# Attention of a hybrid encoder block on one core: score maxima, exponentials and splits issued one slot after their matmuls, queries and keys fetched by head, w_ada sums kept in PSUM

## The chip, the core and the metric

The kernel runs on one core of a Trainium2 chip. The core has a matrix engine (TensorE, PE in the profile; its weight loads are PEld), VectorE (DVE), ScalarE (ACT), GpSimd (POOL), and a queue (SP) from which nearly all transfers are started. Sixteen DMA engines carry those transfers between the chip's memory and SBUF. Matmuls write to PSUM, which VectorE and ScalarE read. The metric is the device time of one execution in microseconds (us), the median over several runs.

## What is computed

One encoder block over a sequence of 1024 positions of width 1024, all in float32. The part that the change bears on is this:

```python
ada = jax.nn.silu(c) @ w_ada[i] + b_ada[i]
shift1, scale1, gate1, shift2, scale2, gate2 = [t[:, None, :] for t in jnp.split(ada, 6, axis=-1)]
h = rmsnorm(x, g_mix[i]) * (1 + scale1) + shift1
proj = h @ w_in[i]
qa, ka, va, qb, kb, vb, ga, gb = jnp.split(proj, split_at, axis=-1)
oa = mixture_of_dilations(heads(qa, 8), heads(ka, 8), heads(va, 8), rel_bias)
ob = neighbourhood_attention_2d(heads(qb, 8), heads(kb, 8), heads(vb, 8), na_rpb[i])
...
merged = jax.nn.sigmoid(ga) * ya + jax.nn.sigmoid(gb) * yb
x = x + gate1 * (merged @ w_out[i])
```

The dilated attention has eight heads of 64. Each query sees a band of keys at three dilations (1, 4 and 16), each band has its own softmax, and the three results are weighted by the denominators of the three. The neighbourhood attention has eight heads of 64 as well: positions form a grid of 16 by 64, and a query sees a window of 8 by 16 with a learned bias. After this come two branch products, w_out, and a gated feed-forward network with a convolution over three positions, w_up and w_down.

## The kernel before

**Numbers.** TensorE multiplies in a reduced float32 format (fp32r in the profile). To keep full precision each operand is split into a high part (a copy, rounded by ScalarE) and a low part (source minus high part, by VectorE or GpSimd), and a product is three matmuls: high by high, high by low, low by high. So a lot of copy-and-subtract pairs surround every matmul.

**Stages up to the attention.** Rows of w_ada are read in pairs and summed with weights on VectorE, to give ada (`row_pairs`, L671 and L673). Each sum runs over eight rows in a tile `sq` in SBUF and is folded by transposes and reductions afterwards. Beside that TensorE forms the values v (`v_wide`, L308 to L310), which go to a scratch in memory. `t_split` (L765 copy, L766 subtraction) splits sums of blocks of h; these are operands of `p_products`, which forms the queries and keys by a block scheme with seven products for eight (L499 to L501). Its operands are weights, split in `a_operands`. The queries and keys, high and low, are stored in a scratch `q_scr` (`qks` in the profile; 8 pairs of heads, 4 kinds, 128 rows for two heads, 1024 positions): L378 for the dilated heads, L396 for the others.

**The attention** is a list of 100 slots. Each slot holds lists of jobs named first, O, T, late O, S, last and W, and `run` issues them in this order; between them `fill` issues steps of another product, the gate projections gA and gB (three matmuls of 512 columns a step, L84 to L86), so that TensorE has work while softmaxes run. `catch_up`, called behind each fill, issues queued small jobs: splits of values (`v_tile`), additions of an output's halves (`finish`, L920 and L921) and splits of gate weights. The instructions of TensorE, ScalarE and VectorE stand in exactly the order in which the code issues them here; SP's and GpSimd's are ordered by a scheduler.

- A **dilated head** takes eight slots from s0. In slots s0 to s0+3 far scores are formed (`far_scores`, L987 and L988, four matmuls, high queries stacked on low ones against keys), in s0+4 to s0+7 near scores (L1027, L1028) that use queries in another order (`qb`, rearranged by GpSimd in `q_blocks`). With the scores, in the same slot, comes the softmax: VectorE takes the maximum (L877), ScalarE the exponential (L878). Two slots later the probabilities P are turned on TensorE (L999, L1044, tile T), and at once split (`split_t`, L885 on ScalarE to `th`, L886 on VectorE to `tl`); another slot later `far_out` and `near_out` (L1011, L1061) multiply them with the values.
- A **pair** of dilated heads shares statistics (maxima and denominators). They are turned, stored to memory, loaded in another shape (`fs`, L1093 and L1099), made into factors (L1105 onwards), stored and loaded again (`fb`, L1134) and multiplied onto the outputs (L1139).
- A **neighbourhood head** takes four slots. Its scores (L1197) are added to a bias that is fetched for each block (`bias`, L1183, two buffers); VectorE takes the minimum of the negated sums (L1201), ScalarE the exponential (L1203); GpSimd divides (L1210), TensorE turns (L1219) and multiplies with the values (L1232).

**Loads of queries and keys.** `qk_load` fetches one pair of heads: per head one transfer for the queries (`qs`, L402, high and low at once) and four for the keys (`ks` and `kl`, L405, each twice so that both halves of the partitions hold them):

```python
sp.dma_start(f(qk[0][i]), q_scr[pr, 0:2, a])
for y in range(2):
    for b in range(2):
        sp.dma_start(f(qk[1 + y][i])[64 * b:64 * b + 64], q_scr[pr, 2 + y, a])
```

Four buffers of each tile hold two pairs. The first pair is fetched before the last product of `p_products` has ended, the others eight slots ahead of their first head, one pair in every 16 slots in the dilated part and one in every 8 in the other.

The slots' loop, with its number of fills, is

```python
n = 2 if s < 64 else 4 if s < 72 else 3 if s < 88 else 2
...
for job in run(slots[s]["T"]):
    job()
...
run(slots[s]["late O"])
run(slots[s]["S"])
```

and is preceded by five fills (`FIRST`). What the jobs of T return are their splits, which so follow their turn in the same slot.

## Time and profile before

| | |
|---|---|
| runs | 1653.1, 1657.18, 1653.93 us |
| median | 1653.93 us |
| the profiled execution, its own time | 1656.75 us |
| its span in the profile | 1654.9 us |
| mean granted TensorE clock | 0.951 |
| memory traffic | 244.27 MB, 148 GB/s over the span |

The profile shows one execution by hardware records. The busy time of an engine leaves out waits and instructions that only steer or start transfers. PEclk is the clock that was granted to TensorE, 1 (or 9 in the page's tenths) being full. In the views of waits a line says which instruction waited, "<-" for whom, and then the sum in us, how often, and the longest wait. In a timeline a row is one instruction: its start in us from the span's start, its duration in us, engine, line, operation, output and inputs, size, and in brackets the wait ahead of it with who ended it. In a group the number behind "x" is the count of instructions, then busy time in us and mean ns of one, then idle time in front of them.

### The profile page before, as it was taken

The page shows a single profiled execution, that of the slowest core. Times are in us where ns is not written, and L with a number is a line of the kernel's source. Part 1 is how long each engine was busy: PE and PEld are TensorE (multiplying, and loading weights), DVE is VectorE, ACT ScalarE, POOL GpSimd, SP SyncE. Part 2 cuts the span into 40 slices and gives each one's busy share as a digit, 9 for nine tenths or more (in the row PEclk, how much of TensorE's full clock was granted, in tenths as well). Part 3 has the DMA queues.
Part 4 walks back from the last instruction along what each step waited for, and adds up shares of the span by engine and source line. Part 5 has one row for each costly group of instructions (what it writes and reads, how often), then busy time and mean ns, then how long its engine had stood idle before and what let it go on. Part 6 is the DMA issues. An engine that isn't in the chain of part 4 may idle for free.

```text
span 1654.9 us, 21287 instructions
## 1 busy us (share of the span) xinstructions
PE 1496.4 (90%) x7308; PEld 1250.3 (76%) x7308; DVE 985.8 (60%) x1805; ACT 782.6 (47%) x1463; POOL 851.8 (51%) x694
## 2 busy tenths in 40 slices
PE   9999999586879568569999999999999999999998
PEld 8877788465767457468888888788888888888888
DVE  7799543143545334346566268966666656977864
ACT  6514332254655444346643455444444443765642
POOL 4066664322433114244222586777766668689723
PEclk9999999798899788879999999999999999999999
DMA  9575354744537566665586342232222223454312
GB/s 371 189 279 183 97 209 148 196 127 121 152 101 173 164 163 149 164 172 162 195 273 229 129 148 93 89 102 77 77 90 77 97 94 121 132 177 134 105 45 102
DMA packets 131187, 244.27 MB, mean 148 GB/s; under 512 B 47460, under 2 KB 60388, under 8 KB 131044
## 3 DMA queue, kind: packets, MB, share of 16 engines
q1 hardware_dynamic: 129080, 239.97, 46.5%
q10 hardware_dynamic: 2000, 2.95, 0.5%
q8 instruction: 58, 0.95, 0.3%
q14 instruction: 49, 0.40, 0.1%
HBM read 188.74 MB, written 59.90 MB: 150 GB/s over the span
## 4 chain that ended last, share of the span: by engine, by line
PE 58%; DMA 22%; DVE 6%; ACT 5%; POOL 4%; issue 2%; SPq 2%; DVEq 0%; ACTq 0%; POOLq 0%
PE pj L499 12%; PE pj L501 12%; PE pj L500 12%; DMA qs<-qks 5%; PE pj L84 5%; PE pj L86 5%; PE pj L85 5%; DMA bias<-na_bias 4%; DMA qks<-qs 2%; DMA gs<-gs 2%; DMA wraw<-w_in 1%; DMA fb<-fcs 1%; DMA sts<-fs 1%; PE O L1232 1%; DVE tl L886 1%
## 5 line engine op out<-in xcount | busy, mean ns | idle before, releaser
L61 POOL TENSOR_TENSOR wlo<-wraw,whi 128x512 fp32r<-128x512 f32 (+1 forms) x92 | 116.7, 1290 | 142.2 <-ACT whi L57 140.4
L886 DVE TENSOR_TENSOR tl<-T,th 128x512 fp32r<-128x512 f32 (+3 forms) x120 | 76.9, 653 | 140.6 <-ACT th L885 140.5
L500 PE MATMUL pj<-op,wsh 128*128 128x512 f32 x408 | 158.7, 389 | 0.5 <-DVE op L1468 0.5
L499 PE MATMUL pj<-op,wsh 128*128 128x512 f32 x408 | 158.4, 389 | 0.3 <-ACT wsh L57 0.3
L501 PE MATMUL pj<-op,wsl 128*128 128x512 f32 x408 | 157.3, 389 | 0.0
L61 POOL TENSOR_TENSOR wsl<-big,wsh 128x512 fp32r<-128x512 f32 (+1 forms) x86 | 111.2, 1315 | 44.4 <-ACT wsh L57 39.4
L84 PE MATMUL pj<-h,whi 128*128 128x512 f32 x272 | 123.5, 454 | 0.0
L86 PE MATMUL pj<-h,wlo 128*128 128x512 f32 x272 | 113.2, 416 | 0.0
L85 PE MATMUL pj<-h,whi 128*128 128x512 f32 x272 | 113.0, 415 | 0.0
L878 ACT ACTIVATE P<-P,st 128x256 f32<-128x256 f32 x128 | 64.1, 501 | 90.6 <-DVE st L877 90.6
L1678 DVE SCALAR_TENSOR_TENSOR big<-pj,sm,big 128x512 f32<-128x512 f32 (+2 forms) x183 | 94.9, 563 | 16.5 <-ACT big L1672 15.5
L1210 POOL TENSOR_SCALAR P<-P,stb 128x288 f32<-128x288 f32 (+1 forms) x32 | 40.5, 1265 | 107.2 <-DVE stb L1207 61.4
L499 PE MATMUL pj<-op,whi 128*128 128x512 f32 x232 | 90.7, 391 | 0.0
L501 PE MATMUL pj<-op,wlo 128*128 128x512 f32 x232 | 90.3, 389 | 0.0
L500 PE MATMUL pj<-op,whi 128*128 128x512 f32 x232 | 90.3, 389 | 0.0
L500 PEld LDWEIGHTS pj<-op,wsh 128*128 128x128 f32 x408 | 76.6, 188 | 16.8 <-DVE op L1468 0.9
L499 PEld LDWEIGHTS pj<-op,wsh 128*128 128x128 f32 x408 | 76.6, 188 | 16.5 <-ACT wsh L57 0.7
L501 PEld LDWEIGHTS pj<-op,wsl 128*128 128x128 f32 x408 | 76.6, 188 | 16.1 <-POOL wsl L61 0.2
L61 POOL TENSOR_TENSOR wsl<-wraw,wsh 128x384 fp32r<-128x384 f32 (+1 forms) x46 | 56.8, 1255 | 57.1 <-ACT wsh L57 52.8
L1203 ACT ACTIVATE P<-P,stb 128x288 f32<-128x288 f32 (+1 forms) x64 | 36.4, 569 | 99.2 <-DVE stb L1201 99.2
L57 ACT ACTIVATE whi<-wraw 128x1024 fp32r<-128x1024 f32 (+2 forms) x49 | 48.5, 994 | 67.9 <-PE pj L85 30.4
L1672 ACT ACTIVATE big<-pj,sm 128x512 f32<-128x512 f32 x61 | 47.0, 772 | 53.3 <-DVE pj L520 32.0
(473 smaller groups left out, 4649.0 us busy)
## 6 DMA issues: line engine op xcount, KB each, us to landing
wada<-w_ada SPq DMA_DIRECT2D x31, 512.0 KB
qks<-qs SPq DMA_DIRECT2D x28, 512.0 KB
wraw<-w_in SPq DMA_DIRECT2D x26, 512.0 KB
big<-w_up SPq DMA_DIRECT2D x22, 512.0 KB
wraw<-w_up SPq DMA_DIRECT2D x22, 512.0 KB
big<-as SPq DMA_DIRECT2D x22, 512.0 KB
as<-big SPq DMA_DIRECT2D x21, 512.0 KB
qs<-qks SPq DMA_DIRECT2D x16, 512.0 KB
```

What stands on the lines that cost most here:

```text
L57: act.activation(hi, raw, AF.Copy)
L61: lo_eng.tensor_tensor(lo[:, i:i + step], raw[:, i:i + step], f(hi)[:, i:i + step], OP.subtract)
L84: pe.matmul(psum, whi[:, k0 + k], mhi, start=k == 0, stop=False)
L85: pe.matmul(psum, whi[:, k0 + k], mlo, start=False, stop=False)
L86: pe.matmul(psum, wlo[:, k0 + k], mhi, start=False, stop=k == n - 1)
L499: pe.matmul(psum, whi[:, k], bhi, start=j < 4 and k == 0, stop=False, skip_group_check=True)
L500: pe.matmul(psum, whi[:, k], blo, start=False, stop=False, skip_group_check=True)
L501: pe.matmul(psum, wlo[:, k], bhi, start=False, stop=k == n - 1, skip_group_check=True)
L878: act.activation(pp, pp, AF.Exp, bias=mi, scale=-1.0, accum_out=li)
L886: dve.tensor_tensor(tl[:m, :n], pt[:m, :n], f(th)[:m, :n], OP.subtract)
L1672: act.activation(y[:, halves[hf]], src, AF.Identity, bias=conv[:, 3, t:t + 1], scale=conv[:, 1, t:t + 1])
L1678: dve.scalar_tensor_tensor(y[:, dst], src, wt, y[:, dst], OP.mult, OP.add)
```

## The change

Seven things are edited, all before or in the attention; the code behind it is the same but for line numbers.

1. **Softmaxes and splits.** `far_scores`, `near_scores` and the neighbourhood's `scores` now put the softmax on a list `scored`, and `split_t` puts its two halves on a list `turned`. `settle`, called at the start of the next slot, issues first the copies to `th`, then the softmaxes, then the subtractions to `tl`. The outputs follow their turn by two slots instead of one, and a slot's order is first, O, T, fill, S, last, fills. There are 102 slots.
2. **Fills.** One ahead of the slots instead of five; then 2 and 3 in turn in a dilated slot (2 before), 3 in slots 64 to 67, 2 up to slot 95, 1 at the end.
3. **Queries and keys by head.** `qk_load` takes one head and allocates one tile each of `qs`, `ks`, `kl` in a new pool with two buffers. It runs eight slots before a dilated head and four before a neighbourhood head (slot 57 for the first of these). The transfers have the same shapes and number. The first head's load, its biases and its values are issued behind all of `p_products`, in an order written out by hand.
4. **Buffers.** P 6 instead of 5, th and tl 5 instead of 3, bias 3 instead of 2.
5. **Values.** A dilated head's values are fetched three slots before it, apart from its bias; a neighbourhood head's two slots into it, and its division comes two slots after its scores.
6. **Sums of w_ada rows.** The running sum stands in a PSUM tile (`pcol` and `pbc` in turn); the eighth addition writes to `sq` in SBUF.
7. **Splits of sums of h.** ScalarE makes a second copy of each source in PSUM (`pj`), from which VectorE subtracts in all 16 cases (GpSimd did four). The first product's operands are prepared in steps 4 to 7 of the loop over v, not behind the splits.

```diff
-    def qk_load(pr):
-        qk = qk_tiles()
-        for i in range(2):
-            a = slice(64 * i, 64 * i + 64)
-            sp.dma_start(f(qk[0][i]), q_scr[pr, 0:2, a])
-            for y in range(2):
-                for b in range(2):
-                    sp.dma_start(f(qk[1 + y][i])[64 * b:64 * b + 64], q_scr[pr, 2 + y, a])
+    def qk_load(head):
+        pr, i = divmod(head, 2)
+        qk = [qk2.tile([128, S], FR, name=n) for n in ("qs", "ks", "kl")]
+        a = slice(64 * i, 64 * i + 64)
+        sp.dma_start(f(qk[0]), q_scr[pr, 0:2, a])
+        for y in range(2):
+            for b in range(2):
+                sp.dma_start(f(qk[1 + y])[64 * b:64 * b + 64], q_scr[pr, 2 + y, a])
         return qk
...
                 if i == 0:
-                    sums[j] = early.tile([128, 512], FT, name="sq", bufs=2)
+                    sums[j] = ps_n.tile([128, 512], FT, name=("pcol", "pbc")[j % 2])
                 for t, w in enumerate(rows.pop(n), 2 * i):
-                    col = cs[:, t:t + 1]
+                    col, acc = cs[:, t:t + 1], sums[j]
+                    if t == KT - 1:
+                        sums[j] = early.tile([128, 512], FT, name="sq", bufs=2)
                     if t == 0:
-                        dve.tensor_scalar(sums[j], w, col, None, OP.mult)
+                        dve.tensor_scalar(acc, w, col, None, OP.mult)
                     else:
-                        dve.scalar_tensor_tensor(sums[j], w, col, sums[j], OP.mult, OP.add)
+                        dve.scalar_tensor_tensor(sums[j], w, col, acc, OP.mult, OP.add)
...
-        PREP = ()
+        PREP = (4, 5, 6, 7)
...
+                prep = [a_operands(raw.pop(0), 4, p_home, p_sts[0], spot=p_spot)]
...
-        def t_split(n, tp, src, eng):
+        def t_split(n, tp, src):
...
+                copy = ps_g.tile([128, 512], FT, name="pj")
+                act.activation(copy, src[k // 2][:, k % 2], AF.Copy)
                 act.activation(t[:, 0], src[k // 2][:, k % 2], AF.Copy)
-                eng[k % 2].tensor_tensor(t[:, 1], src[k // 2][:, k % 2], f(t)[:, 0], OP.subtract)
+                dve.tensor_tensor(t[:, 1], copy, f(t)[:, 0], OP.subtract)
...
+    qk2 = tc.alloc_tile_pool(name="qk2", bufs=2, reuse_waits="tile")
     sm_pool = tc.alloc_tile_pool(name="sm", bufs=2, reuse_waits="tile")
...
+    with tc.manual_schedule(engines={sp.engine, pool.engine}):
+        qks = {0: qk_load(0)}
...
+        biases = {0: dil_bias(0)}
+        values = {0: v_raw(va_load, 0)}
+        biases[1] = dil_bias(1)
...
+        q_blocks(qks[0])
...
-    def split_t(pt, m=128, n=512):
-        th, tl = (at_pool.tile([128, 512], FR, name=x_, bufs=3) for x_ in ("th", "tl"))
-        act.activation(th[:m, :n], pt[:m, :n], AF.Copy)
-        dve.tensor_tensor(tl[:m, :n], pt[:m, :n], f(th)[:m, :n], OP.subtract)
-        return th, tl
-
+    turned, scored = [], []
+
+    def split_t(pt, then, m=128, n=512):
+        def one():
+            tt = [at_pool.tile([128, 512], FR, name=x_, bufs=5) for x_ in ("th", "tl")]
+            act.activation(tt[0][:m, :n], pt[:m, :n], AF.Copy)
+            return tt
+
+        def two(tt):
+            dve.tensor_tensor(tt[1][:m, :n], pt[:m, :n], f(tt[0])[:m, :n], OP.subtract)
+            then(tt)
+        turned.append((one, two))
+
+    def settle():
+        ts = [(one(), two) for one, two in turned]
+        for job in scored:
+            job()
+        for tt, two in ts:
+            two(tt)
+        turned.clear()
+        scored.clear()
+
+    qks[1] = qk_load(1)
...
+                at(s0 - 8, "first", lambda: qks.update({self.head: qk_load(self.head)}))
+            if self.head:
+                at(s0 - 3, "first", self.load_v)
                 at(s0 - 2, "first", self.prepare)
...
                 at(s0 + n, "S", self.far_scores, n)
                 at(s0 + n + 2, "T", self.far_turn, n)
-                at(s0 + n + 3, "late O", self.far_out, n)
+                at(s0 + n + 4, "O", self.far_out, n)
                 at(s0 + n + 4, "S", self.near_scores, n)
...
-                    at(s0 + n + 6, "W" if js == (8,) else "T", self.near_turn, js)
-                    at(s0 + n + 7, "late O", self.near_out, js)
+                    at(s0 + n + 6 + (js == (8,)), "T", self.near_turn, js)
+                    at(s0 + n + 8 + (js == (8,)), "O", self.near_out, js)
...
+            at(57 if head == 0 else s0 - 4, "first", lambda: qks.update({8 + head: qk_load(8 + head)}))
+            at(s0, "first", self.begin)
+            at(s0 + 2, "first", self.load)
+            at(s0 + 4, "last", self.prepare)
...
-                at(s0 + n + 1, "first", self.normalise, cb)
+                at(s0 + n + 2, "first", self.normalise, cb)
...
-    fill(FIRST)
-    for s in range(100):
-        n = 2 if s < 64 else 4 if s < 72 else 3 if s < 88 else 2
+    fill(1)
+    for s in range(102):
+        n = 2 + s % 2 if s < 64 else 3 if s < 68 else 2 if s < 96 else 1
+        settle()
         run(slots[s]["first"])
         run(slots[s]["O"])
...
+        run(slots[s]["T"])
+        fill(n > 1)
         run(slots[s]["S"])
         run(slots[s]["last"])
-        fill(n > 3)
-        for job in run(slots[s]["W"]):
-            job()
-        fill(1)
+        fill(n - (n > 1))
```

Three places of the order show what moves. The first is TensorE in the middle of a dilated head. T are turned probabilities, pj a fill, O an output, S scores. Before:

```order
L999 MATMUL T<-idt,P 128x128 x4
L84 MATMUL pj<-h,whi 128x512
L85 MATMUL pj<-h,whi 128x512
L86 MATMUL pj<-h,wlo 128x512
L1011 MATMUL O<-th,vv 128x256
L1011 MATMUL O<-tl,vv 128x256
L1011 MATMUL O<-th,vv 128x256
L1011 MATMUL O<-tl,vv 128x256
L1027 MATMUL S<-ks,qb 128x256
L1028 MATMUL S<-kl,qb 128x256
```

and now:

```order
L1034 MATMUL O<-th,vv 128x256
L1034 MATMUL O<-tl,vv 128x256
L1034 MATMUL O<-th,vv 128x256
L1034 MATMUL O<-tl,vv 128x256
L1022 MATMUL T<-idt,P 128x128 x4
L84 MATMUL pj<-h,whi 128x512
L85 MATMUL pj<-h,whi 128x512
L86 MATMUL pj<-h,wlo 128x512
L1049 MATMUL S<-ks,qb 128x256
L1050 MATMUL S<-kl,qb 128x256
```

Output O before was that of the turn T issued one slot earlier; now it is that of a turn two slots earlier and stands at the slot's head.

The second place is the queue SP where the projections end and the attention begins. qks<-qs are stores of queries and keys, qs, ks and kl<-qks the loads, vv the values of a head. Before:

```order
L378 DMA qks<-qs 128x2x512
L402 DMA qs<-qks 128x1x1024 x2
L378 DMA qks<-qs 128x2x512
L65 DMA wraw<-w_in 128x1024
L405 DMA kl<-qks 64x1024
L405 DMA ks<-qks 64x1024 x2
L405 DMA kl<-qks 64x1024
L405 DMA ks<-qks 64x1024 x2
L405 DMA kl<-qks 64x1024 x2
L378 DMA qks<-qs 128x2x512
L851 DMA lnm<-ln_mult 128x384
```

and now:

```order
L375 DMA qks<-qs 128x2x512 x2
L65 DMA wraw<-w_in 128x1024
L375 DMA qks<-qs 128x2x512 x2
L399 DMA qs<-qks 128x1x1024
L402 DMA ks<-qks 64x1024 x2
L402 DMA kl<-qks 64x1024 x2
L849 DMA lnm<-ln_mult 128x384
L692 DMA bias<-p_bias 128x512
L693 DMA bias<-p_bias 128x384
L680 DMA vv<-v 128x8x64
```

One head is loaded instead of two, behind the last store instead of between the stores; the second head's load comes after both heads' biases.

The third place is VectorE among the sums over rows of w_ada (mt is the fold that follows a sum):

```order
 L190 TENSOR_REDUCE mt<-idt 128x32
-L671 TENSOR_SCALAR sq<-wada,cs 128x512
-L673 SCALAR_TENSOR_TENSOR sq<-wada,cs,sq 128x512 x7
+L670 TENSOR_SCALAR pcol<-wada,cs 128x512
+L672 SCALAR_TENSOR_TENSOR pcol<-wada,cs,pcol 128x512 x6
+L672 SCALAR_TENSOR_TENSOR sq<-wada,cs,pcol 128x512
 L181 STREAM_TRANSPOSE mt<-sq 128x512
 L185 TENSOR_REDUCE mt<-mt 128x16
```

Seven additions of eight rows read and wrote a tile in SBUF; now all seven read PSUM, six of them write it, and the seventh writes SBUF.

More of the change, by code (lines that the diff above doesn't have):

```diff
@@ L362, in hybrid_encoder @@
     q_scr = dram.tile([8, 4, 128, S], FT, name="qks")
-    def qk_tiles():
-        return [[qkpool.tile([128, S], FR, name=n) for _ in range(2)] for n in ("qs", "ks", "kl")] + [[]]
     def split_qk(y, dst, src):
@@ L840, in hybrid_encoder @@
                 next(nxt, None)
-            if n + 1 == len(order) and j == 2:
-                qk = qk_load(0)
     first_w = w_split(ahead.pop(24), pool)
-    for i in range(2):
-        q_blocks(qk, i)
     ps.release()
@@ L848, in hybrid_encoder @@
     lpool.release()
+    qkpool.release()
+    qk2 = tc.alloc_tile_pool(name="qk2", bufs=2, reuse_waits="tile")
     sm_pool = tc.alloc_tile_pool(name="sm", bufs=2, reuse_waits="tile")
-    lnm = sm_pool.tile([128, 384], FT, name="lnm", bufs=1)
-    sp.dma_start(lnm, ln2_mult)
-    loads = [dil_loads(head) for head in range(2)]
+    with tc.manual_schedule(engines={sp.engine, pool.engine}):
+        qks = {0: qk_load(0)}
+        lnm = sm_pool.tile([128, 384], FT, name="lnm", bufs=1)
+        sp.dma_start(lnm, ln2_mult)
+        biases = {0: dil_bias(0)}
+        values = {0: v_raw(va_load, 0)}
+        biases[1] = dil_bias(1)
+        pool.tensor_tensor(biases[0][:, 512:896], biases[0][:, 512:896], lnm, OP.add)
+        q_blocks(qks[0])
     ps_l = tc.alloc_tile_pool(name="psl", bufs=2, space=PSUM, reuse_waits="tile")
     ps_a = tc.alloc_tile_pool(name="psa", bufs=2, space=PSUM, reuse_waits="tile")
-    def finish_o(po, dst):
-        act.activation(dst, po[64:128], AF.Copy)
-        dve.tensor_tensor(dst, po[0:64], dst, OP.add)
     def block_chunks(b):
@@ L1016, in near_scores @@
         def near_scores(self, n):
-            qs, ks, kl, qb = qks[self.pr]
+            ks, kl, qb = qks[self.head][1:]
             i, st = self.i, self.st()
             s = ps_l.tile([128, 512], FT, name="S")
-            P = sm_pool.tile([128, 2, 256], FT, name="P", bufs=5)
             for x_ in range(2):
@@ L1162, in __init__, with begin @@
                 at(s0 + n, "S", self.scores, cb)
-                at(s0 + n + 1, "first", self.normalise, cb)
+                at(s0 + n + 2, "first", self.normalise, cb)
             for n, pair in enumerate(((0, 3), (1, 2))):
-                s = s0 + 3 + 2 * n
+                s = s0 + 4 + 2 * n
                 for y in range(3):
                     at(s + (y == 2), "T", self.turn, pair, y)
-                at(s + 2, "O", self.out, pair)
+                at(s + 3, "O", self.out, pair)
+        def begin(self):
+            self.st = at_pool.tile([128, 2, 8], FT, name="stb", bufs=3)
         def load(self):
@@ L1172, in load @@
                 oTs[self.head // 2] = at_pool.tile([128, S], FT, name=("u1", "u23")[self.head // 2 % 2])
-            self.st = at_pool.tile([128, 2, 8], FT, name="stb")
             self.vv = v_raw(vb_load, self.head)
@@ L1274, in fill_steps @@
             w = w_next
-    def qk_ahead(pr):
-        qks[pr] = qk_load(pr)
-    qks, oTs = {0: qk}, {}
-    loads = dict(enumerate(loads))
+    oTs = {}
     for pr in range(4):
@@ L1284, in hybrid_encoder @@
         NaHead(head, 64 + 4 * head)
-    for n, cb in zip((52, 55, 59, 61), (0, 3, 1, 2)):
+    for n, cb in zip((54, 56, 59, 61), (0, 3, 1, 2)):
         at(n, "first", vb_chunks, cb)
-    for pr in range(1, 8):
-        at(16 * pr - 8 if pr < 5 else 8 * pr + 24, "first", qk_ahead, pr)
     steps = fill_steps()
```

140 lines of the change are left out of this document (67 added, 73 removed).

## The prediction

> **What bounds the kernel now.** I read the page's summary and slices first, then the busy times of a few stretches, then who waits for whom on each engine, and last the timeline around the longest waits.
>
> ```profile
> PE 1496.4 (90%) x7308; PEld 1250.3 (76%) x7308; DVE 985.8 (60%) x1805; ACT 782.6 (47%) x1463; POOL 851.8 (51%) x694
> ...
> PE   9999999586879568569999999999999999999998
> ...
> PEclk9999999798899788879999999999999999999999
> DMA  9575354744537566665586342232222223454312
> GB/s 371 189 279 183 97 209 148 196 127 121 152 101 173 164 163 149 164 172 162 195 273 229 129 148 93 89 102 77 77 90 77 97 94 121 132 177 134 105 45 102
> ```
>
> TensorE is the busiest engine and is full from slice 20 on. It is open in slices 8 to 19, where its clock falls too and the DMA share is highest. Those slices are the end of the projections and the attention. The same in microseconds (columns: stretch, its length, then busy time and instructions of each engine, clock, DMA share, GB/s):
>
> ```profile
> core 0: us, PE busy (x) PEld busy (x) DVE busy (x) ACT busy (x) POOL busy (x), PEclk, DMA share, GB/s
> ...
> 276.00:310.00 34.00, 21.91 (x98) 17.86 (x96) 4.77 (x7) 1.95 (x4) 8.87 (x10) 0.86 0.53 147
> 310.00:593.00 283.00, 214.46 (x1207) 179.02 (x1207) 122.56 (x397) 148.04 (x406) 78.30 (x72) 0.88 0.57 149
> 593.00:747.00 154.00, 103.00 (x538) 88.21 (x538) 62.76 (x185) 61.45 (x164) 49.78 (x45) 0.81 0.60 158
> 747.00:800.00 53.00, 49.91 (x312) 43.84 (x311) 33.19 (x102) 35.73 (x96) 29.49 (x26) 0.99 0.59 179
> 800.00:1655.00 855.00, 845.11 (x3868) 702.49 (x3866) 574.12 (x881) 415.86 (x606) 535.15 (x436) 0.99 0.37 122
> ```
>
> The borders are those of the program, seen in the first score matmul of a stage and in two of the waits:
>
> ```profile
> 309.86 0.55 PE L987 MATMUL S<-ks,qs 128*128 128x256 f32 x1 [12.09 <-DMA ks<-qks]
> 322.97 1.39 PE L999 MATMUL T<-idt,P 128*128 128x128 f32 x4 [7.55 <-ACT P L878]
> 592.69 0.29 PE L1197 MATMUL S<-ks,qs 128*128 128x288 f32 x1
> 746.99 0.29 PE L1197 MATMUL S<-ks,qs 128*128 128x288 f32 x1
> ```
>
> Slot 0 of the attention begins at 309.86, slot 64 (first neighbourhood head) at 592.69, and counting score matmuls, four to a slot, slot 84 at 746.99. So 64 dilated slots take 283 us, 20 neighbourhood slots 154 us (31 us a head), and the last 16 slots 53 us (3.3 us each, 13 us a head). What comes after 800 us holds TensorE at 845 of 855 us; the change does not touch it. TensorE's own waits in the attention:
>
> ```profile
> PE S L1197 <- DVE stb L1201: 36.3, 5, 10.4
> PE O L1011 <- ACT th L885: 19.0, 3, 7.1
> PE O L1061 <- DVE tl L886: 18.7, 7, 11.1
> PE O L1061 <- ACT th L885: 13.5, 2, 12.7
> PE S L987 <- DMA ks<-qks: 12.1, 1, 12.1
> PE T L1044 <- ACT P L878: 10.7, 1, 10.7
> PE T L999 <- ACT P L878: 8.0, 4, 7.6
> ```
>
> Together 118 us, in few pieces of 5 to 13 us. In between, slots flow. VectorE and ScalarE, which are named, are idle more than half of this time, so their own work is not what is late. What they wait for:
>
> ```profile
> DVE P L1201 <- DMA bias<-na_bias: 60.5, 8, 13.8
> DVE u L1139 <- DMA fb<-fcs: 22.4, 6, 11.5
> DVE fl L1105 <- DMA fs<-sts: 19.4, 3, 7.2
> ...
> 375.81 0.60 ACT L1269 ACTIVATE gs<-pj 128x512 f32<-128x512 f32 x1 [12.20 <-DMA gs<-gs]
> ...
> SPq L695 <- DMA qs<-qks: 40.6, 4, 11.0
> SPq L1183 <- DMA qs<-qks: 26.3, 3, 8.9
> ```
>
> All are transfers, and the queue SP that issues them stood still for one kind, qs<-qks. That transfer is slow by itself:
>
> ```profile
> 346.00:356.00 10.00, 8.68 (x54) 7.16 (x53) 5.60 (x18) 5.94 (x19) 5.79 (x6) 1.00 0.13 50
> ...
> qs<-qks SPq DMA_DIRECT2D x16, 512.0 KB
> ```
>
> Here it runs nearly alone: 50 GB/s at a DMA share of 0.13, that is 2 of 16 engines. Its 512 KB so take 10.5 us on two engines, and whatever is spread over all 16 ends behind it on these two. **The bound of the attention is this pair of DMA engines**, 16 times 10.5 us plus their part of the rest.
>
> [...]
>
> **The change, part by part.**
>
> *Score maxima, exponentials and splits one slot later.* No instruction is added; P tiles go from 5 to 6, th and tl from 3 to 5. The chains PE S, DVE, ACT, PE T and PE T, ACT, DVE, PE O get a slot each. What the edit can remove is waiting for short chains; what it cannot remove is TensorE's work. That is 214.46 x 0.88 / 64 = 2.95 us of full clock a dilated slot with two fills. A fill is three matmuls; their price:
>
> ```profile
> 1160.00:1200.00 40.00, 40.00 (x178) 33.14 (x177) 25.53 (x40) 16.79 (x21) 28.04 (x22) 1.00 0.24 80
> ```
>
> 40 us / 178 = 0.225 us each, 0.67 us a fill. The new schedule has 2.5 fills in a dilated slot instead of 2, so its floor is 2.95 + 0.34 = 3.29 us, 64 x 3.29 = 211 us.
>
> Of the dilated 283 us, 189 are TensorE's work (64 x 2.95) and about 54 are long waits: 22.4 for fb, 19.4 for fs, 12.2 for gs. The other 40 are low clock and short waits. Afterwards I put: 211 work; 20 of the short waits (half; bounds 0 and 40); fs 9 and fb 18. The gs wait goes, as it came from two qs loads back to back, which loading by head does not give. Sum 258, a gain of **25 us**. Why fs and fb stay: the transfers of the pair's statistics are as before, and their chain is long:
>
> ```profile
> 401.21 0.47 SPq L1093 DMA_DIRECT2D sts<-fs  x1
> ...
> 407.51 2.88 SPq L1099 DMA_DIRECT2D fs<-sts  x8
> ...
> 411.63 0.18 DVE L1105 TENSOR_TENSOR fl<-fs 64x32 f32<-64x32 f32 x1 [7.18 <-DMA fs<-sts]
> ```
>
> From issue to use 10.4 us. The rows are now copied a slot later while factors stays at slot 20, so the lead is about 2.5 slots, 8 us, where it was 3.4. 3 us of wait a pair remain even if no qs load is ahead. An fb wait is a wait in VectorE's queue: behind it stand all maxima and splits, and TensorE is held one slot later than now.
>
> *Queries and keys by head.* The same 16 loads with the same bytes, two buffers of each tile instead of four, 8 slots ahead (4 in the neighbourhood stage). Now four heads are fetched before slot 64, so that only four loads fall in the 154 us; afterwards seven fall in slots 64 to 88. The bias has three buffers and its reader comes a slot later. Floor on the two hot engines for a dilated head: share 0.57 x 283 = 161 us, less ten qs loads (10 x 10.5 x 2/16 = 13), over 8 heads 18.5, plus 10.5 = 29 us, 233 us for eight: below my 258. For a neighbourhood head: from the last stretch 0.59 x 53 / 4 = 7.8, plus the 1 MB of ks and kl (3.8 us at the 279 GB/s of the page's third slice, which is full of spread loads), plus 10.5 = 22 us; from the stretch before, (0.60 x 154 - 6) / 5 + 10.5 = 28 us, with the fills and statistics it held. I take 24, the last stretch's row being nearer in fills. Seven heads at 24 and ten slots at 3.3 make 201, plus 2 us of slack at the last loads; now 207 (592.69 to 800). With VectorE's 60.5 us of bias waits gone in part but more loads, I count **6 us** of gain. Bounds: 187 (22 a head) and 229 (28 a head).
>
> *Start.* The first pair's loads no longer stand ahead of the last qks stores, and one head (one hot load) comes before slot 0 instead of two. Of the waits of 12.09 and 7.55 us I take half, **9 us**; bounds 0 and 19. POOL's q blocks fall from eight to four there.
>
> *Sums of w_ada rows and splits in PSUM.* 42 additions read their running sum from PSUM, 16 splits a copy that ScalarE makes there.
>
> ```profile
> L673 DVE SCALAR_TENSOR_TENSOR sq<-wada,cs,sq 128x512 f32<-128x512 f32 x42 | 48.9, 1164 | 4.7 <-DMA wada<-w_ada 3.3
> ...
> L766 DVE TENSOR_TENSOR op<-qs,op 128x512 fp32r<-128x512 f32 x6 | 8.2, 1412 | 0.0
> ...
> L208 DVE SCALAR_TENSOR_TENSOR pv<-wada,cs,pv 128x512 f32<-128x512 f32 x6 | 4.5, 753 | 0.1
> ...
> L886 DVE TENSOR_TENSOR tl<-T,th 128x512 fp32r<-128x512 f32 x54 | 37.3, 691 | 83.6 <-ACT th L885 83.6
> ...
> 100.90 0.76 PE L309 MATMUL pv<-vwl,h 128*128 128x512 f32 x1 [3.79 <-DVE vwl L61]
> 139.49 0.50 PE L308 MATMUL pv<-vwh,h 128*128 128x512 f32 x1 [2.89 <-ACT vs L315]
> ```
>
> With a PSUM operand the same operations take 753 and 691 ns instead of 1164 and 1412: VectorE saves 42 x 0.41 + 11 x 0.72 = 25 us, less four splits taken over from GpSimd (3 us). TensorE waited only these two times longer here, so at most 7 us come out; I take **4**. The 16 copies (about 0.6 us each, 10 us) lie in ScalarE's idle time of that stage; without that cover they would cost the 10. The first product's operands, which are now prepared during the v products (steps 4 to 7) and not behind the splits, add no instruction; GpSimd and ScalarE do them beside TensorE's v products, and I take nothing, between the 3.8 us of the longer wait above either way.
>
> [...]
>
> Sum: 25 + 6 + 9 + 4 = 44 us. The profiled execution took 1656.75 us (span 1654.9), so 1612.75; the three runs have their median 2.8 us lower, at 1653.93, and I give **1610 us**.
>
> **The rivals.**
>
> *Floor of the hot engines* (pipelining pays fully): dilated 233, neighbourhood 187, 19 + 7 at the edges: 50 + 20 + 26 = 96 us, 1558. For it: the 40 us of short waits are what the edit aims at. Against it: statistics chains and eight transfers at most ahead of SP keep the hot engines from being always fed.
>
> *The loads do not bind* (each hides in eight slots): 211 + 20 and 38 x 3.3 = 125: 52 + 82 + 13 = 147 us, 1507. Against it stands the DMA share of 0.13 at 50 GB/s.
>
> *Just in time becomes too late, slower than before.* Two buffers and a lead of four slots, 13 us, cannot hold a load that needs 10.5 us on engines with other work in line. Should a neighbourhood head with its own load take the 31 us of today's, seven of them and ten slots make 250 us, 43 more than now; it decides from 31 - 13 = 18 us of waiting a head. With dilated slots gaining 15 (the same lateness on vv, three slots ahead and behind a qs load) and 9 + 4 at the edges the time is 1654 + 15 = 1669. For it: L1201's waits, which are of this kind. Against it: three bias buffers and a later reader.
>
> *The waits only move*: dilated slots trade 25 us for 15 in fb and fs, no gain in the neighbourhood stage, 13 at the edges: 1630.
>
> **How the numbers follow.** Forecast 1610 with its own range 1590 to 1622: 0.42. Floor of the hot engines 1558: 0.18. Loads do not bind 1507: 0.07. Waits only move 1630 (to 1648): 0.17. Late loads: 0.16, a fifth of it within 5 us of no change. About 0.3%, 5 us, is what a measurement here can tell from no change. So faster 0.81, same 0.06, slower 0.13. Leaving out the two ends, the range is 1548 to 1655.
>
> **What would show it.** Right: first dilated score near 300 us, dilated stage near 258 us, VectorE's waits on na_bias halved, L672 near 750 ns, and SP still standing at qs<-qks. Wrong: neighbourhood heads at 31 us or at 13, waits on fs or fb that grow beyond 40 us, ScalarE held by vv, or time lost after the attention, where I expect the same 855 us.

## The result and the profile after

The changed kernel takes 1638.18 us (median of 4 runs, 1636.94 to 1639.49) against 1654.04; the ratio is 0.9901, with an interval of 0.9884 to 0.9918. It is faster by 16 us, about 1%, where 44 us were forecast. The profiled execution took 1637.79 us (span 1635.6), 19 less than that of before. Its summary and slices:

```profile
PE 1477.8 (90%) x7308; PEld 1248.2 (76%) x7308; DVE 961.3 (59%) x1809; ACT 791.8 (48%) x1479; POOL 838.7 (51%) x690
...
PE   9999998578989846567999999999999999999998
...
PEclk9999999789989867878999999999999999999999
DMA  9584445554644757665776441222222223444312
```

TensorE is open in slices 7 to 19 (8 to 18 before), and the clock is low in nearly the same places. The borders of the stages, from TensorE's timeline (first score of a dilated head, first of a neighbourhood head, last output):

```profile
302.06 0.55 PE L1006 MATMUL S<-ks,qs 128*128 128x256 f32 x1 [19.95 <-DMA ks<-qks]
562.10 0.29 PE L1225 MATMUL S<-ks,qs 128*128 128x288 f32 x1
...
787.50 0.28 PE L1267 MATMUL O<-tl,vv 128*128 128x128 f32 x1
```

and the busy times between them (columns as in the prediction):

```profile
core 0: us, PE busy (x) PEld busy (x) DVE busy (x) ACT busy (x) POOL busy (x), PEclk, DMA share, GB/s
673.70:753.30 79.60, 50.19 (x288) 44.50 (x289) 32.95 (x103) 34.90 (x95) 27.78 (x25) 0.80 0.64 167
562.00:787.50 225.50, 145.33 (x815) 127.97 (x814) 97.37 (x290) 96.45 (x258) 76.85 (x68) 0.80 0.59 153
302.00:562.00 260.00, 220.84 (x1294) 194.19 (x1295) 122.24 (x397) 149.51 (x411) 85.58 (x81) 0.91 0.55 151
```

The last output before came at 809.07 us:

```profile
809.07 0.28 PE L1232 MATMUL O<-tl,vv 128*128 128x128 f32 x1
```

| us | before | after | gain |
|---|---|---|---|
| TensorE empty ahead of slot 0 (start of the wait for the first keys) | 297.8 | 282.1 | 15.7 |
| that wait | 12.1 | 20.0 | -7.9 |
| dilated stage, first score to first neighbourhood score | 282.8 | 260.0 | 22.8 |
| neighbourhood stage, to the last output | 216.4 | 225.4 | -9.0 |
| the rest | 845.8 | 848.1 | -2.3 |

The sum is 19.3, the difference of the two spans. Of the 15.7 us, 2.7 are four fills of 0.67 us that now lie in the slots. The neighbourhood stage, forecast to gain, lost; from first score to first score its seven heads took 27.4, 35.6, 26.0, 28.8, 26.9, 26.6 and 26.9 us, 198 in all. TensorE's, VectorE's and SP's largest waits show where:

```profile
PE T L1254 <- DVE tl L890: 57.8, 8, 11.8
PE T L1022 <- DVE tl L890: 21.2, 6, 7.9
PE S L1006 <- DMA ks<-qks: 20.0, 1, 20.0
```

```profile
DVE P L1235 <- DMA bias<-na_bias: 88.9, 9, 13.0
```

```profile
SPq L774 <- DMA qs<-qks: 32.0, 5, 8.7
```

VectorE's waits for the bias, which were to be halved, grew from 60.5 to 88.9 us. TensorE waits for a split (tl), but the split only stands in VectorE's queue behind a sum that waits for its bias. The bias has not come because SP stood still ahead of it. SP's queue during one head (start, duration, transfer):

```profile
677.60 0.55 SPq L399 DMA_DIRECT2D qs<-qks  x1
678.20 0.47 SPq L402 DMA_DIRECT2D ks<-qks  x1
678.72 1.23 SPq L402 DMA_DIRECT2D kl<-qks  x2
680.05 0.53 SPq L1213 DMA_DIRECT2D bias<-na_bias  x1
680.67 0.38 SPq L65 DMA_DIRECT2D wraw<-w_in  x1
681.28 2.06 SPq L1213 DMA_DIRECT2D bias<-na_bias  x1
683.43 14.39 SPq L774 DMA_DIRECT2D vv<-v  x4
697.92 2.52 SPq L1213 DMA_DIRECT2D bias<-na_bias  x2
```

The slow load of the queries is issued at 677.6, and SP stands at the loads of values from 683 to 698, with the next two biases behind. Of these 14.4 us, 8.7 (the longest in the line above) are a wait for the queries to land, 17.5 us after their issue. VectorE's wait is three links from its cause.

### The profile page after: what moved, and what is told of

It reads as the page before. It is cut to its first block, busy times and chain, and to the rows that moved or that the text cites. A ratio compares the mean times of both kernels' runs of the same rounds, so it can differ in the third digit from the quotient of the medians.

```text
span 1635.6 us, 21337 instructions
## 1 busy us (share of the span) xinstructions
PE 1477.8 (90%) x7308; PEld 1248.2 (76%) x7308; DVE 961.3 (59%) x1809; ACT 791.8 (48%) x1479; POOL 838.7 (51%) x690
## 4 chain that ended last, share of the span: by engine, by line
PE 45%; DVE 3%; POOL 2%; ACT 1%; issue 1%; DMA 1%; DVEq 0%; SPq 0%; POOLq 0%; ACTq 0%
PE pj L496 10%; PE pj L497 10%; PE pj L498 10%; PE pj L86 5%; PE pj L84 4%; PE pj L85 4%; POOL wlo L61 0%; POOL wsl L61 0%; DMA oraw<-w_ada 0%; ACT whi L57 0%; DVE op L1598 0%; DMA wraw<-w_down 0%; DVE wlo L61 0%; PE pcol L108 0%; ACT op L1597 0%
## 5 line engine op out<-in xcount | busy, mean ns | idle before, releaser
L1697 DVE SCALAR_TENSOR_TENSOR big<-pj,sm,big 128x512 f32<-128x512 f32 (+2 forms) x183 | 94.9, 563 | 16.5 <-ACT big L1691 15.5
L875 DVE CUSTOM_DVE_ANT_0 P<-S,bias 128x256 f32<-128x256 f32 x128 | 49.1, 420 | 85.9 <-PE S L1007 36.3
L1235 DVE CUSTOM_DVE_ANT_0 P<-S,bias 128x288 f32<-128x288 f32 (+1 forms) x64 | 30.3, 506 | 114.3 <-DMA bias<-na_bias 88.9
L1254 PE MATMUL T<-idt,P 128*96 128x128 f32 (+1 forms) x192 | 33.9, 312 | 68.9 <-DVE tl L890 57.8
```

Source lines behind the costliest of these rows:

```text
L875: dve.tensor_tensor_reduce(pp, d, bias, -1.0, BIG, OP.add, OP.min, mi)
L1697: dve.scalar_tensor_tensor(y[:, dst], src, wt, y[:, dst], OP.mult, OP.add)
```

## The experiments

Stages are read as in the table above, each from one profiled execution; ratios are to the kernel before, with intervals.

| run | what differs | us | ratio | first score | dilated | neighbourhood |
|---|---|---|---|---|---|---|
| before | | 1654.0 | 1 | 309.9 | 282.8 | 216.4 |
| after | | 1638.2 | 0.9901 | 302.1 | 260.0 | 225.4 |
| e1 | after, queries spread | 1516.3 | 0.9161 (0.9139 to 0.9184) | 291.9 | 214.5 | 157.7 |
| e2 | before, queries spread | 1547.0 | 0.9353 (0.9339 to 0.9368) | 296.6 | 226.9 | 170.0 |
| e3 | after, 3 load buffers, 8 slots ahead | 1645.3 | 0.9937 (0.9912 to 0.9962) | 303.0 | 275.0 | 217.5 |
| e4 | after, splits in their slot | 1633.6 | 0.9876 (0.9855 to 0.9898) | 303.9 | 253.9 | 224.1 |
| e5 | after, early part undone | 1647.9 | 0.9965 (0.9951 to 0.9978) | 314.1 | 258.3 | 222.6 |
| e6 | after, splits of h undone | 1639.8 | 0.9916 (0.9890 to 0.9943) | 304.3 | 258.4 | 222.4 |
| e7 | before, calls by head | 1656.4 | 1.0017 (0.9998 to 1.0036) | 305.9 | 285.4 | 215.0 |
| e8 | e1, splits in their slot | 1518.1 | 0.9177 (0.9153 to 0.9201) | 291.1 | 209.5 | 163.7 |
| e9 | e4, outputs one slot earlier | 1637.5 | 0.9891 (0.9859 to 0.9924) | 302.5 | 264.6 | 217.9 |
| e10 | after, 2 bias buffers | 1641.5 | 0.9916 (0.9886 to 0.9945) | 301.7 | 256.6 | 231.6 |
| e11 | e1, 14 fills first | 1522.8 | 0.9198 (0.9171 to 0.9226) | 292.7 | 211.7 | 166.5 |
| e12 | e1, 3 load buffers, 8 slots ahead | 1513.9 | 0.9142 (0.9109 to 0.9175) | 291.9 | 214.7 | 158.3 |
| e13 | after, fills of before | 1627.2 | 0.9822 (0.9792 to 0.9851) | 303.1 | 244.8 | 225.4 |
| e14 | before, fills of after | 1652.1 | 0.9993 (0.9973 to 1.0014) | 308.5 | 284.3 | 206.0 |
| e15 | 4 load buffers | 1676.3 | 1.0133 (1.0104 to 1.0163) | 302.4 | 288.2 | 231.4 |
| e16 | e1, fills of before | 1505.9 | 0.9092 (0.9069 to 0.9116) | 292.0 | 194.9 | 165.6 |
| e17 | e15 with 2 load buffers | 1665.9 | 1.0069 (1.0047 to 1.0092) | 303.0 | 262.1 | 246.7 |
| e18 | after, th and tl 4 | 1637.4 | 0.9904 (0.9868 to 0.9940) | 303.8 | 258.0 | 224.2 |

**The slow transfer (e1, e2).** The one load of queries is cut into two of 64 partitions:

```diff
-        sp.dma_start(f(qk[0]), q_scr[pr, 0:2, a])
+        for x_ in range(2):
+            sp.dma_start(f(qk[0])[64 * x_:64 * x_ + 64], q_scr[pr, x_, a])
```

> The changed kernel, but the queries of a head come in two transfers of 64 partitions x 1024 (high, low), as the keys do, instead of one whose source has two rows outermost. Bytes are the same, 16 transfers more. Theory (the two busy DMA engines bound the attention: SP stood 42 us at qs<-qks in the neighbourhood stage, a head took 26.5 us there): a neighbourhood head falls to 16 to 18 us (DMA share 0.6 x 26.5 = 16), the dilated stage from 260 to 215 to 230 us, the wait for the first keys from 20 to 12 us; together 1530 to 1565 us. Rival (two buffers and a lead of four slots are too short whatever the transfer's speed): heads stay over 23 us and the time over 1615 us.

> The kernel before with the same edit of the queries' transfer alone. Theory (two busy engines): its waits for bias, fb, fs and gs, 115 us together, mostly go: 1550 to 1590 us. By the rival that the splits' order holds the kernel before: over 1630 us. Beside the changed kernel with the same edit it shows what the change is worth without the slow transfer: 20 to 40 us if the slots' order pays by itself, under 10 us if the change only dealt with the slow transfer.

Measured: 122 us less in the changed kernel, 106 in the one before, more than either expectation. Windows of e1 ahead of slot 0 and in the dilated stage:

```profile
284.00:292.00 8.00, 0.09 (x1) 0.12 (x1) 0.00 (x0) 0.00 (x0) 0.00 (x0) 0.75 0.97 241
291.90:506.40 214.50, 208.79 (x1294) 185.18 (x1295) 124.94 (x397) 148.50 (x412) 85.77 (x81) 0.99 0.74 188
```

The first loads run at a DMA share of 0.97, where the slow load by itself had 0.13; TensorE is busy in 209 of 214.5 us at a clock of 0.99. In the changed kernel, which keeps the transfer's shape, the load is as slow as before: from 294 to 302 us, ahead of slot 0, the DMA share is 0.14 at 55 GB/s. The two stages are 45.5 and 67.7 us shorter than in the changed kernel. So this load, on its two engines (0.13 of 16), held back the attention in both kernels. These two runs don't tell how much of that is the two engines being full and how much is SP standing until the load has landed, since the spread transfer ends both. Without the slow load the change is worth 30.6 us, nearly twice what it is with it.

**Lead and buffers in the neighbourhood stage (e3, e10).**

```diff
-    qk2 = tc.alloc_tile_pool(name="qk2", bufs=2, reuse_waits="tile")
+    qk2 = tc.alloc_tile_pool(name="qk2", bufs=3, reuse_waits="tile")
...
-            at(57 if head == 0 else s0 - 4, "first", ...
+            at((55, 58, 64)[head] if head < 3 else s0 - 8, "first", ...
```

> The changed kernel with three buffers of qs, ks, kl and the neighbourhood heads' loads eight slots ahead instead of four (th and tl have 4 buffers for 5 to make room). Theory (two busy engines, and SP's queue standing at their landing with values and bias behind): heads stay at 25 to 28 us and the time within 6 us of 1638. Rival (the lead of four slots is too short): heads at 16 to 20 us, 1580 to 1600 us.

> The changed kernel with two buffers of the bias instead of three. Theory (the neighbourhood heads run at the pace of the two busy DMA engines, whose 26.5 us a head no bias buffer changes): neighbourhood stage within 6 us of 225, time 1632 to 1645. Rival (the third bias buffer is what kept the heads from the 30 us that they took before): heads at 29 to 31 us, time 1655 to 1670.

In e3 the third to sixth heads still take 26 to 29 us, and only the seventh, whose load is done, takes 15.5. A longer lead doesn't help these heads. It moves a load (ten instead of nine start there) into the dilated stage, which grows by 15 us; the time, 7 us longer, lies just outside the theory's 6. With two bias buffers the time moves by no more than the intervals allow; from the third on, heads take 27 to 29 us, and the stage, 231.6 us, is a little over the 6 us that the theory allowed it.

**The slot's order (e4, e8, e9).** e4 settles in the slot itself; e9 also puts the outputs of the dilated heads one slot behind their turn.

```diff
-        settle()
         run(slots[s]["first"])
         run(slots[s]["O"])
         run(slots[s]["T"])
+        settle()
         fill(n > 1)
         run(slots[s]["S"])
+        settle()
```

> The changed kernel, but maxima, exponentials and splits follow their matmuls in the same slot again (settled behind T and behind S); everything else, the outputs two slots after their turn too, stays. Theory (the later slot took the short waits away): the dilated stage goes from 260 back to 275 to 283 us, and the time to 1653 to 1665 us. Rival (loads by head made the 23 us): dilated stage within 5 us of 260, time within 8 us of 1638.

> The changed kernel with the queries' transfer spread over 64 partitions twice, and maxima, exponentials and splits in the slot of their matmuls again. Theory (the later slot pays once the slow transfer is gone, since short chains are then what TensorE waits for; 12 us in the dilated stage between the two kernels with spread queries): dilated stage 222 to 230 instead of 214.5 us, time 1526 to 1540 instead of 1516 us. Rival (the later slot pays nothing here either): within 5 us of 1516.

> The changed kernel with the slot's order of the kernel before: maxima, exponentials and splits in the slot of their matmuls, and a dilated head's outputs one slot behind their turn, between the fill and the scores. Theory (the outputs' second slot took the short waits away, since undoing the place of the splits alone changed nothing): dilated stage 270 to 283 us, time 1650 to 1662. Rival (no part of the slots' order counts; fs waits 6 instead of 19 us and no gs wait come from the loads' order and the longer slots): dilated stage within 6 us of 257, time 1630 to 1644.

In time all three came out by the rival; e9's dilated stage, 264.6 us, lies 2 us above the rival's bound, and e4's, 253.9, 1 us below it. Settling one slot later, the edit that the title names first, is worth nothing that can be measured, with the slow load or without it.

**The early part (e5, e6).** e5 has the removed lines of `row_pairs` and `t_split` and `PREP = ()` again, e6 those of `t_split` and `PREP` alone.

> The changed kernel with the early part undone: sums of w_ada rows in SBUF, splits from SBUF (a quarter on GpSimd), the first product's operands prepared behind the splits. Theory (the projections ended 13.0 us earlier by this part and the wait for the first keys, 20.0 us, is counted from their end): TensorE runs empty at 295 instead of 282 us, time 1648 to 1654 us. Rival (the prediction's 4 us are right, and the rest came from the first pair's loads no longer standing between the stores): TensorE empty at 284 to 288, time 1640 to 1645 us.

> The changed kernel with the splits of sums of h and the early preparation undone, the sums of w_ada rows still in PSUM. Theory (5.3 us of the 13.0 had come by the end of the products with the values, the other 7.7 in the first products, by the splits and the early preparation): TensorE empty at 288 to 291 us, time 1643 to 1648 us. Rival (the sums alone make the 13 us, the splits nothing): empty at 282 to 284, time 1636 to 1640 us.

In e5 TensorE runs empty at 314.1 - 20.7 = 293.4 us, 11.3 later than in the changed kernel, and the time is 9.7 us longer, six tenths of what the change brings. In e6 it runs empty at 284.0. The sums make 9.4 of the 11.3 us. The other 1.9 can't be put down to the splits and the preparation: the runs that have them, with one fill ahead of slot 0, run empty at 281.9 to 283.9 us. e6 came out by its rival, and e5 within 2 us of its theory.

**Loads by head in the kernel before (e7).** Only the slots of the calls were changed.

> The kernel before, but queries and keys fetched by head at the slots of the changed kernel (eight ahead, in the neighbourhood part four, slot 57 for its first head), with its four buffers; the first pair stays as it was. Theory (the sixteen slow transfers only change stages: eight instead of ten fall in the dilated slots): the dilated stage falls from 283 to 260 to 268 us, the neighbourhood stage grows from 216 by 5 to 20 us, time within 10 us of 1654. Rival (loading by head leaves the dilated stage as it was, the changed kernel's 23 us come from its order of slots): dilated stage over 277 us.

This one did not do what it says: SP's order is made by the scheduler, which starts a load when a buffer is free. The sixteen loads started at nearly the same times as before (325, 332, 380, 411 us against 328, 335, 383, 413). It tells nothing of loading by head; buffers had to be changed for that.

**Fills (e13, e14, e11, e16).**

```diff
-    fill(1)
+    fill(5)
...
-        n = 2 + s % 2 if s < 64 else 3 if s < 68 else 2 if s < 96 else 1
+        n = 2 if s < 64 else 4 if s < 72 else 3 if s < 88 else 2 if s < 99 else 0
```

> The changed kernel with the fills of the kernel before (5 ahead, 2 in a dilated slot, then 4, 3, 2). Theory (longer slots hide the statistics' way through memory: VectorE's waits for fs 6 to 10 us instead of 19): fs waits return to 15 to 22 us and the dilated stage stays at 255 to 265 us although 28 fills fewer lie in it; with those fills in the neighbourhood stage the time is 1640 to 1652 us. Rival (the dilated stage is TensorE's work and a fixed number of waits): dilated stage 238 to 248 us, neighbourhood stage longer by what was moved, time within 6 us of 1638.

> The kernel before with the fills of the changed one (1 ahead, 2 and 3 in turn in dilated slots, 3 in slots 64 to 67, then 2). Theory (longer slots hide the statistics' way): fs waits 5 to 12 instead of 19 us, dilated stage 270 to 283 us with 28 more fills in it, neighbourhood stage 195 to 210, time 1635 to 1648. Rival (fills change places only): dilated stage 295 to 305 us, neighbourhood stage 195 to 205, time within 6 us of 1654.

In e13 the dilated stage has 32 fills fewer (128 against 160) and is 15.2 us shorter; four of them stand ahead of slot 0 and 28 in the neighbourhood stage, which has the same 225.4 us. The first is the rival's forecast, the second neither's, and the time lies below both. So in the changed kernel fills are free where heads wait for the slow load, and cost most of their time in the dilated stage: moving them forward cost the change 11 us. In the kernel before (e14) it was the other way: the dilated stage had room for them (284.3), the neighbourhood stage got 10 us shorter in the profile, and the time did not move beyond its interval, as its rival had it. VectorE's waits for fs in the dilated stage are 8.6 us in e13 and 18.4 in e14, so longer slots aren't what shortens them.

> The changed kernel with the spread transfer of the queries, and 14 fills instead of 1 ahead of slot 0, taken from slots 64 to 67 and 87 to 95. Theory (TensorE stands idle for 9.0 us for the first keys, which 13 fills of 0.67 us cover, and the later slots wait for transfers and not for fills): 1507 to 1513 instead of 1516 us. Rival (what is filled ahead is missing behind, where short chains then show): 1514 to 1520 us.

> The changed kernel with the spread transfer of the queries and the fills of the kernel before (5; 2 in a dilated slot; 4, 3, 2). Theory (the dilated stage is TensorE's work, 28 fills of 0.67 us fewer shorten it by 15 to 19 us, while the neighbourhood heads wait for transfers part of their time and take in about half of them): dilated stage 195 to 200, time 1500 to 1510. Rival (without the slow transfer fills cost the same everywhere): 1513 to 1520.

Fills ahead of slot 0 (e11) took the wait for the first keys away, but the neighbourhood stage grew by 9 us, all of it from the last head on, where 9 fills stand for 12 and TensorE waits 7.5 us for values; the time, 1522.8 us, is no better than e1's and above both expectations. Fewer fills in dilated slots (e16) made 1505.9 us, 132 less than the changed kernel and the lowest of all. e12, with a longer lead on top of e1, expected

> The changed kernel with the spread transfer, three buffers of qs, ks, kl and the neighbourhood heads' loads eight slots ahead (th and tl have 4 buffers). Theory (with the slow transfer gone the first neighbourhood heads, 25 and 26 us against 15 to 16 later, are held by transfers that crowd there at a DMA share of 0.84, which an earlier load spreads): neighbourhood stage 145 to 152 instead of 158 us, time 1504 to 1512. Rival (they are held by the fb and values transfers, which this doesn't move): within 5 us of 1516.

and is no different from e1 within the intervals; the rival was right.

**What shortened the dilated stage (e15, e17, e18).** e15 has four load buffers and pairs' loads; to make room P, th, tl and bias have their old numbers and the slots their old order. e17 is e15 with two load buffers and loads by head, so these two differ in both. e18 is e3's partner: it has e3's four buffers of th and tl, but the changed kernel's load buffers and lead.

> The changed kernel with four buffers of qs, ks and kl and a pair's two loads at the slots of the kernel before; to make room P has 5 buffers, th and tl 3, the bias 2, and maxima, splits and outputs stand in the slots of the kernel before. Only the early part, the fills, the start and the order of the values' loads stay as changed. Theory (two buffers hold a slow load back until a pair's statistics are through; four let it start ahead of them): dilated stage 272 to 285 us, neighbourhood stage 205 to 218. Rival (the count of buffers doesn't matter): dilated stage 255 to 266 us, neighbourhood stage 218 to 228.

> The kernel of e15 with two buffers of qs, ks and kl and the loads by head at the changed kernel's slots; P, th, tl, bias and the slots' order as in e15. Theory (the load buffers decide): dilated stage 255 to 266 us, against 288 in e15; time 1640 to 1655. Rival (the smaller buffers of P, th and tl decide): dilated stage 278 to 292 us, time 1665 to 1680.

> The changed kernel with th and tl at 4 buffers. Theory (the load buffers decide): dilated stage 255 to 264 us as with 5, against 275 in e3; time within 5 us of 1638. Rival (th and tl decide): dilated stage 270 to 278 us.

First neighbourhood score of e15 and of e17, whose first dilated scores stand within 0.6 us of each other:

```profile
590.63 0.29 PE L1225 MATMUL S<-ks,qs 128*128 128x288 f32 x1
```

```profile
565.05 0.29 PE L1225 MATMUL S<-ks,qs 128*128 128x288 f32 x1
```

e18 came out by its theory. Two buffers with loads by head, instead of four with loads by pair, shorten the dilated stage by 26 us; two, instead of three with the longer lead (e18 against e3), by 17. By e7 the slots of the loads alone change nothing where there are four buffers. What the buffers do is seen in the starts of the slow loads. With four buffers (e15) eleven start from slot 0 to slot 64, three of them close together (326.9, 330.5, 345.1 us); with two (e17) nine, none less than 20 us behind the one before it. Behind the three, SP stood for 10 us at a store of gate projections; the third load landed at 372.8, 27.7 us after its start, and the store 0.6 us after that. ScalarE in e15 waits for the store as in the kernel before (12.20 us at 375.81 there):

```profile
373.55 0.60 ACT L1304 ACTIVATE gs<-pj 128x512 f32<-128x512 f32 x1 [17.72 <-DMA gs<-gs]
```

In the dilated stage such waits make 30.5 us in e15 and 10.5 in e17, 20 of the 26 us between them:

```profile
ACT gs L1304 <- DMA gs<-gs: 30.5, 3, 17.7
```

```profile
ACT gs L1304 <- DMA gs<-gs: 10.5, 1, 10.5
```

e15's neighbourhood stage missed its expectation (231 us, not 205 to 218), and its dilated stage lies 3 us above its own. e17's dilated stage came out by the theory, but its time by the rival, 1665.9 us, because its neighbourhood stage is 21 us longer than the changed kernel's. There TensorE waits 78.2 us in 15 pieces for values, which are fetched as late as in the changed kernel but used one slot sooner. So in that stage the larger buffers and the later output, taken together, do pay; they were not tried one by one, except the bias.

## Why the forecast was wrong in size

- **The bound** was named rightly: the queries' load on two DMA engines. e1 and e2 show it with 122 and 106 us. Term by term, 25 + 6 + 9 + 4 us were forecast, and the spans show 22.8 - 9.0 - 7.9 + 13.0, with 2.7 of fills and -2.3 of the rest, 19.3 in all. Two terms failed and came out with the other sign: the neighbourhood head and the start.
- **The neighbourhood head.** The forecast put 24 us between bounds of 22 and 28, as the last stretch's row was "nearer in fills", and ten quick slots behind. The heads took 26.5 us (79.6 / 3) once steady, none under 26, and 28.3 in the mean of seven: 198 us instead of 168. By the same sum with the row of the steady stretch: 0.64 x 26.5 = 17.0 us of all engines, less 1.3, plus 10.5 gives 26.2. By this estimate both engines are full there; in the trace's packet records fewer than two transfers are under way in 3% of that stretch (12% of the whole stage). What was mis-sized is the two engines' other work: 7.8 + 3.8 = 11.6 us a head in the forecast, 17.0 - 1.3 = 15.7 by this row. The row of the kernel's own middle (28) was nearer than its end, where no slow load ran any more (the last began at 715.5). "6 us of gain" became a loss of 9; the sum with its own 2 us of slack gave 4, and its "now 207" ended at 800 us, 9 us ahead of the last output. Fills, by which the row was chosen, do not count in this stage of the changed kernel (e13).
- **The start.** Half of two waits, 9 us, was to go. The wait for the first keys grew from 12.1 to 20.0 instead, a miss of 17 us and about as large as the other. All loads now come behind the projections: the first queries' load starts at 283.3 (274.6 before) while TensorE runs empty 15.7 us earlier, and it is as slow as before (a share of 0.14 from 294 to 302 us); e1 cuts the wait to 9.0. The second wait, at 322.97, lies inside the dilated stage, whose sum had it already; it went, but TensorE now waits 10.1 us for values at 351.3, and ScalarE's waits for values in that stage, named as a sign of being wrong, grew from 4.1 to 38.4 us. Slot 0 came near 300 us as forecast, for another reason, the early part.
- **The early part** was put at 4 us, capped by TensorE's two waits of 7 us, and came out at 10 to 13. The price of an addition was right:

```profile
L672 DVE SCALAR_TENSOR_TENSOR pbc<-wada,cs,pbc 128x512 f32<-128x512 f32 x18 | 13.6, 756 | 2.5 <-DMA wada<-w_ada 1.9
L672 DVE SCALAR_TENSOR_TENSOR pcol<-wada,cs,pcol 128x512 f32<-128x512 f32 x18 | 13.6, 755 | 0.6
```

  The reason was not. 1164 ns before was the mean of two kinds of additions (durations as least / median / most):

```profile
L673 DVE SCALAR_TENSOR_TENSOR sq<-wada,cs,sq x42: 741/752/2773, 74.6 to 150.0; 128x512 f32<-128x512 f32 x42
```

```profile
L672 DVE SCALAR_TENSOR_TENSOR pcol<-wada,cs,pcol x18: 745/756/757, 74.7 to 135.2; 128x512 f32<-128x512 f32 x18
```

  From SBUF, too, an addition takes 752 ns at the median. The slow ones, 14 of 42 with 1.65 to 2.77 us, are those that ran beside GpSimd's work, as these four did:

```profile
108.76 11.12 DVE L673 SCALAR_TENSOR_TENSOR sq<-wada,cs,sq 128x512 f32<-128x512 f32 x4
```

```profile
108.53 5.18 POOL L705 TENSOR_TENSOR qs<-qs,ks 128x1024 f32<-128x1024 f32 x2
113.67 2.85 POOL L707 TENSOR_TENSOR ks<-ks,qs 128x1024 f32<-128x1024 f32 x1
116.48 2.84 POOL L707 TENSOR_TENSOR qb<-qb,qs 128x1024 f32<-128x1024 f32 x1
```

  With the running sum in PSUM none of the 42 takes over 757 ns, beside GpSimd or not. The edit takes the additions out of GpSimd's way; it doesn't make an addition faster by itself.

  The cap was wrong. TensorE's loss in that stage lay less in long waits than in short ones and in a lower granted clock (0.90 and 0.97, then 0.97 and 1.00). From 100 to 200 us, before and after:

```profile
100.00:150.00 50.00, 46.06 (x190) 37.05 (x191) 49.04 (x42) 10.77 (x16) 35.05 (x18) 0.90 0.64 227
150.00:200.00 50.00, 45.28 (x186) 35.23 (x186) 31.31 (x35) 21.23 (x35) 36.47 (x26) 0.97 0.26 90
```

```profile
100.00:150.00 50.00, 46.05 (x200) 37.02 (x201) 34.43 (x48) 17.33 (x28) 30.75 (x19) 0.97 0.68 242
150.00:200.00 50.00, 50.00 (x221) 41.42 (x222) 27.02 (x40) 28.38 (x46) 34.66 (x28) 1.00 0.33 116
```

  VectorE was full (49.04 of 50 us) in the first stretch and is at 34 now; busy time times clock is 85 us of TensorE's work before and 95 after. With the running sum in PSUM and in SBUF the medians of an addition, 756 and 752 ns, are 4 ns apart, and e6, which has the sums in PSUM, shows a gain (TensorE empty at 284.0 us, 293.4 in e5).
- **The dilated stage** came out at 260.0 us for a forecast of 258, with VectorE's waits for fs at 6.3 us (9 forecast; another 4.3 now fall behind the stage) and for fb at 19.4 (18), and no gs wait. TensorE's work is 220.84 x 0.91 = 201 us (211), and what is left, low clock and short waits, 33 (20): two misses of 10 and 13 us that cancel by luck.

```profile
DVE u L1165 <- DMA fb<-fcs: 19.4, 6, 6.8
DVE fl L1131 <- DMA fs<-sts: 6.3, 2, 3.9
```

  The reason given was half wrong. That fewer slow loads fall in the stage, and none close behind another, is what e15 and e17 show for the stage's 23 us, as far as buffers and loads by head can be told apart; the later slot took nothing from the stage (e4, e9). But loading by head doesn't remove the gs wait, as the prediction said: e4, e9 and e17 have it too (12.2, 11.5 and 10.5 us), with over 20 us between their slow loads, and they settle in the slot itself. In the changed kernel it is gone, and the stage is no shorter for it.
- **The rest** of 2.3 us lies within what this stretch differs between the runs (848 to 852 in most), and stays unexplained.

Of the rivals, "the waits only move" came nearest in time (1630 to 1648), though its dilated stage was to gain 10 us and gained 23. "Just in time becomes too late" had the sign of the neighbourhood stage, at 28.3 us a head instead of its 31, but not the cause: with a longer lead and a third buffer all heads but the last of the seven stay as slow (e3).

## What to carry to other kernels

Where one transfer keeps a few DMA engines busy, look first at its shape: a line that spreads it was worth over seven times what all these edits brought. Until then many an edit only moves the waiting from stage to stage, and what a buffer or a filler is worth differs with the stage: 32 fills cost one stage 15 us and 28 the other nothing (e13), and four load buffers for a pair, instead of two for a head, lengthened the first by 26 us and shortened the second by 15 (e15 against e17). Before a mean of durations is used as a price, look at its least and its median: here the mean hid what ran beside. When a wait names an engine, follow its queue: here TensorE's wait for a split was VectorE's for a bias, SP's for values, and in the end the queries' load.

## What was not expected of the hardware

- One kind of transfer, sixteen times 10.5 us at a DMA share of 0.13 (two of 16 engines), cost 122 us. With the transfer spread, the time (1516 us) is near the 1507 that the rival "the loads do not bind" had been given; the granted clock rose with it, from 0.91 in the dilated stage to 0.99 in e1's.
- More buffers made a stage slower: 262 us with two load buffers and loads by head, 288 with four and loads by pair, where slow loads that may start early do start, next to others.
- An addition on VectorE with all operands in SBUF took 752 ns while GpSimd was still and 1.65 to 2.77 us beside GpSimd's work; with the running sum in PSUM it took at most 757 ns either way.
